# A diffusion layer on one core: where the sums of weight blocks and two sets of squares are kept and issued

## The chip, the cores and the metric

One core of a Trainium2 chip. The time is the device time of one execution, in microseconds (us), as the median of several runs. A profile is one further execution, with every instruction's start and duration on each engine: TensorE (PE, with its weight loads PEld), VectorE (DVE), ScalarE (ACT), GpSimd (POOL) and the queue of SyncE (SP), which issues most DMAs.

## The reference

One layer of a hybrid diffusion model in fp32: 1024 latent tokens of width 1024, and 256 context tokens that are only read by the latents. Cut to what matters:

```python
x = x + 0.5 * ml[2] * swiglu(modulate(rms_norm(x, norm1_g), ml[0], ml[1]), ffn1_w_in, ffn1_w_out)   # first half step
hx = modulate(rms_norm(x, norm2_g), ml[3], ml[4])
bg, cg, vc, q, k, v, gt = split(hx @ w_in)                       # mixers
y = bg * short_conv(cg * vc, conv_w)
o = attention(rope(rms_norm(q)), rope(rms_norm(k)), v)           # over context and latents
x = x + ml[5] * (sigmoid(g_conv) * (y @ w_bc) + sigmoid(g_attn) * (o @ w_ba)) @ w_out
x = x + 0.5 * ml[8] * swiglu(modulate(rms_norm(x, norm3_g), ml[6], ml[7]), ffn2_w_in, ffn2_w_out)   # second half step
return rms_norm(x, final_g)
```

`swiglu(h, a, b)` is `(silu(h @ a1) * (h @ a2)) @ b` with an inner width of 2816; `ml[i]` are shifts, scales and gates worked out from `silu(c)`. The context tokens `cx` go through the first half step and the keys and values as well.

## The kernel before

**Precision.** Every large product is taken in parts: an operand is cast on ACT to a high part (type fp32r), and DVE subtracts it from the operand for the low part (`split`, line 197). Three matmuls then stand for one: high by high, high by low, low by high.

**Fast products.** The three large products with many columns (ffn1_w_in, the mixers' w_in, ffn2_w_in) and the two with ffn1_w_out and ffn2_w_out use Winograd's form of Strassen's scheme: seven half-sized products, numbered 1 to 7, in place of eight. Their operands are blocks of weights and activations, and sums of such blocks.

*Class `Winograd` (line 491)* does the first three. The activations' operands (`r`, r1 to r7 and r0) are made by `norm0` (line 529, for the first 512 tokens, C0) and `norm1` (line 556, for the second 512, C1; temporaries `nt`, `h22` and `h12`). The weights' operands come from the generator `lefts` (line 617): for each pair of weight column blocks it loads two blocks `a` and `b` (tiles `raw`, a ring of three), makes the sums s1 = b0 + b1, s2 = s1 - a0, s3 = a0 - b0 and later a1 - s2 on POOL, and splits each into a tile of the ring `wl` (four). `prefetch` keeps four such operands ahead of PE.

Products 1 and 2 need only C0, so `start` (line 702) takes them for the first 9 pairs while `norm1` is still at work. Their results u (product 1) and c (products 1 + 2) lie in one tile of the ring `wh`, which has four buffers (`W_BUFS`). The pairs 0 and 1 (`RESIDENT` = 2) stay in it; the others are written to DRAM by `put_aside` (line 716) and loaded back by `fetch` (line 754), one pair ahead of `next_first`. After that every pair takes products 6, 7, 4, 5 and 3 (`second`, `third`), whose results DVE adds to u, v and b. The first half step does the same with its own `start_by_half`.

*`row_products` (line 820)* does the products with the second weights. It runs the seven products in the order 2, 1, 4, 6, 5, 7, 3; each goes through the 11 blocks of rows in six groups (k = 0, 2, ... 10). The right operands (`rh`, `rl`) are split from the blocks of the hidden values (`hid`), the left ones from weights (`raw`) or from weight sums (`ws`) that are built in place by DMAs with addition, issued by POOL (`plus`). In product 3 both operands lie in the rings `wl` and `wh`. After each group and at each product's end a callback `after(i, k)` is called; for the first half step it is `after1` (line 1271). When a set of four rows of `x` is complete, `done` in it writes them to DRAM and calls `mix.square` (line 545) on each: ACT squares the tile into `sq`, and DVE adds it to the accumulator `sq_acc`, from which the next norm's factor is made. `mix.accs` keeps one accumulator for C0 and one for C1.

**Rings.** `ttile` (line 116) gives a tile of 512 fp32 columns from the ring with tag t, which has 11 buffers. `rh`, `rl`, `sq`, `sq_acc`, `nt`, `h22`, `u`, `c`, `v`, `b`, `y`, the sums s1 to s3 and the tiles of the modulation (`rawm`, `macc`) all come from it. PE's results go to banks: five with tag s (`ps`), two with tag t (`pt`), one with tag o (`po`).

**Order.** The kernel is written as straight code, and the framework's planner lays each engine's queue out with a model of the durations: among the instructions that are ready, the one that stands first in the code goes first, and a new tile waits for a free buffer. Instructions marked with `strict` or `pinned` keep the order of the code on their engine. On the chip every engine then works through its queue strictly in that order.

All operations pass through one helper at line 90, so the profile shows L90 nearly everywhere; operations are told apart by the names of their tiles.

Of the kernel before, what the change touches and what calls it, by code (L numbers as in the profile page):

```python
# [9 lines left out]
F32 = mybir.dt.float32  # L10
# [8 lines left out]
P = 128  # L19
# [16 lines left out]
C0, C1, CC = ("l", 0, 512), ("l", 512, 512), ("c", 0, CT)  # L36

A_BUFS = 38
W_BUFS = 4
# [7 lines left out]
RESIDENT, AH2, AH3 = 2, 9, 9  # L47
# [4 lines left out]
def tile_dit_layer(  # L52
# [48 lines left out]
    wpool = ctx.enter_context(tc.tile_pool(name="wpool", bufs=5))  # L101
# [7 lines left out]
    def uniq(s):  # L109
        n_tiles[0] += 1  # L110
        return f"{s}_{n_tiles[0]}"

    def atile(name, shape=(P, SLOT), dt=F32):
        return apool.tile(list(shape), dt, tag="A", name=uniq(name))

    def ttile(name, n=512, dt=F32):
        t = tpool.tile([P, 512], dt, tag="t", name=uniq(name))
        return t[:, :n]
# [13 lines left out]
    def matmul(out, w, x, start, stop, pinned=False, on=False):  # L132

        inst = pe.matmul(out, w, x, start=start, stop=stop, skip_group_check=on)
        if pinned:
            tc.keep_in_program_order(inst)
# [7 lines left out]
    def load(out, in_, pinned=False):  # L144
        inst = sp.dma_start(out=out, in_=in_)
        if pinned:
            tc.keep_in_program_order(inst)
# [49 lines left out]
    def split(src, hi, lo, lo_eng=None, hi_eng=None):  # L197

        if hi_eng is dve:
            dve.tensor_copy(out=hi, in_=src)  # L200
        else:
            act.copy(out=hi, in_=src)
        (lo_eng or dve).tensor_sub(out=lo, in0=src, in1=hi.bitcast(F32))
# [177 lines left out]
    def norm_gain(name, m, gname):  # L381

        g = {}
        for s in "l" if m >= 5 else "lc":
            g[s] = const.tile([P, 8], F32, name=f"{name}_{s}")
            part_gain(g[s], m, gname, s, 0, 8)
        return g
# [77 lines left out]
    def run(steps, n=None):  # L465

        if n is None:
            for _ in steps:
                pass
        else:  # L470
            for _ in range(n):
                next(steps, None)
# [18 lines left out]
    class Winograd:  # L491
# [125 lines left out]
        def lefts(self, pairs, side_from):  # L617

            def cols(src):
                t = wpool.tile([P, SLOT], F32, tag="raw", name=uniq("raw"), bufs=3)  # L620
                load(t[:].rearrange("p (k n) -> p k n", n=P), src.rearrange("(k p) n -> p k n", p=P))
                return t[:, :512], t[:, 512:]

            def half_cols(src, half):
                t = wpool.tile([P, SLOT], F32, tag="raw", name=uniq("raw"), bufs=3)[:, :512]
                src = src[half * 512 : (half + 1) * 512]
                load(t.rearrange("p (k n) -> p k n", n=P), src.rearrange("(k p) n -> p k n", p=P))
                return t

            def parts(src):  # L630
                tag = "wh" if self.side_from and self.n_left < 2 * n + 4 and self.n_left % 2 else "wl"
                self.n_left += 1
                t = wpool.tile([P, 2, 512], F32R, tag=tag, name=uniq(tag), bufs=W_BUFS)
                strict[0] = bool(self.side_from) and self.n_left <= 2 * BY_HALF
                split(src, t[:, 0], t[:, 1], self.lo_eng)
                strict[0] = False
                return t

            n = self.n_ahead
            m = BY_HALF if self.side_from else 0  # L640
            for t in self.halves[:m]:
                yield parts(t)
            for a, _ in pairs[:m]:
                yield parts(half_cols(a, 1))
            for a, _ in pairs[m:n]:
                yield from map(parts, cols(a))
            for j, (wa, wb) in enumerate(pairs):
                side = side_from is not None and j >= side_from
                a, b = cols(wa), cols(wb)
                s1, s2, s3 = ttile("s1"), ttile("s2"), ttile("s3")  # L650
                pool.tensor_add(out=s1, in0=b[0], in1=b[1])
                pool.tensor_sub(out=s2, in0=s1, in1=a[0])
                pool.tensor_sub(out=s3, in0=a[0], in1=b[0])
                if j >= n:
                    yield from map(parts, a)
                yield parts(s2)
                yield parts(s3)
                if side:
                    yield parts(b[0])
                yield parts(b[1])  # L660
                yield parts(s1)
                pool.tensor_sub(out=s2, in0=a[1], in1=s2)
                yield parts(s2)
                if side_from is not None and j == side_from - 1:
                    for wa, wb in pairs[:side_from]:
                        yield from map(parts, cols(wa) + cols(wb))

        def prefetch(self, n, lo_engines=(None, None)):
            while len(self.ready) < n:
                self.lo_eng = lo_engines[len(self.ready) % 2]  # L670
                w = next(self.source, None)
                if w is None:
                    break
                self.ready.append(w)
# [27 lines left out]
        def start(self, norm):  # L702

            for i in range(self.n_ahead):
                t = wpool.tile([P, 2, 512], F32, tag="wh", name=uniq("uc"), bufs=W_BUFS)
                u, c = t[:, 0], t[:, 1]
                act.copy(out=u, in_=self.product(1))
                run(norm, 1)
                dve.tensor_add(out=c, in0=u, in1=self.product(2))
                if i < RESIDENT:  # L710
                    self.started.append((u, c))
                else:
                    self.put_aside(t)
            run(norm)

        def put_aside(self, t):
            ucd = dram.tile([P, 2, 512], F32, name=uniq("ucd"))
            sp.dma_start(out=ucd[:], in_=t[:])
            self.started.append(ucd)
# [308 lines left out]
    def column_pairs(w, offsets):  # L1028
        return [tuple(w[:, o : o + P] for o in ab) for ab in offsets]
# [40 lines left out]
    for k in range(4):  # L1070
# [7 lines left out]
        half1.keep(1, k, h0[k][:, 0])  # L1078
    start = half1.start_by_half()
    run(start, 1)  # L1080
    for k in range(4):
        xt = turned(t0, k + 4, ps_o if k % 2 else ps_t)
# [122 lines left out]
    for j in range(NH):  # L1205
        half1.side = side(j) if j >= SIDE_FROM else None
        u, c = half1.next_first()
# [26 lines left out]
    for d in range(0, KD, 2):  # L1234
        t = ttile("cx")
# [23 lines left out]
    mix = Winograd(xs, None, modl, 3, column_pairs(wi, mix_offsets), plain=True, ahead=AH2)  # L1259
# [8 lines left out]

    residual = {(2, 4): (C0, 0), (1, 6): (C0, 4), (4, 8): (C1, 0), (6, 4): (C1, 4)}

    def after1(i, k):
        def done(ds, ch):
            for d in ds:
                sp.dma_start(out=xd[d, :, ch[1] : ch[1] + 512], in_=xs(d, ch))
                mix.square(d, ch)

        if (i, k) in residual:
            ch, d0 = residual[i, k]
            for d in range(d0, d0 + 4):
                sp.dma_start(out=xs(d, ch), in_=xd[d, :, ch[1] : ch[1] + 512])  # L1280
        if (i, k) == (5, 0):
            gain2.update(norm_gain("gain2", 3, "g2"))
            mix.gain = gain2["l"]
        if k == NH // 2:
            if i == 1:
                done(range(4), C0)
            elif i == 7:
                done(range(4, KD), C0)
                run(norms2, 1)
                done(range(4, KD), C1)  # L1290
            elif i == 3:
                done(range(4), C1)
        if i == 3 and k in (0, 4):
            run(norms2, 1)

    row_products(ffn1_w_out[0], hs, add1, after1)


# [19 lines left out]
    for i in range(KD):  # L1318
        u = atile("u")
# [57 lines left out]
    for kt in range(10):  # L1377
        ch = CC if kt < 2 else C0 if kt < 6 else C1
# [270 lines left out]
    u = units[0]  # L1649
# [127 lines left out]
    for j in range(NH):  # L1777
        if j > 1:
            run(last_steps, 3)
        u, c = fast.next_first()  # L1780
# [82 lines left out]
```

## Time and profile before

| | us |
|---|---|
| median of 3 runs | 2678.27 |
| lowest and highest run | 2674.46 and 2678.47 |
| profiled execution | 2677.21 |
| its span, first to last instruction | 2675.3 |
| PE busy | 2637.8 |
| DVE busy | 2007.0 |
| ACT busy | 1172.3 |
| POOL busy | 557.1 |

A timeline's row gives the start in us from the span's start, the duration, the engine, the operation, `out<-in` by the program's tile names, the shape and the count; in brackets stands the engine's idle time before it and what ended it. Where several instructions of a kind follow one another, a row merges them. A row on waits gives the total, the number of waits and the longest. A row of a stretch gives its length and what each engine was busy in it, with the number of instructions that touch it. Matmuls overlap in the pipeline, so the booked duration of one (0.39 us) is longer than the pitch from one start to the next.

### The profile page before, as it was taken

The page shows a single profiled execution, that of the slowest core. Times are in us where ns is not written, and L with a number is a line of the kernel's source. Part 1 is how long each engine was busy: PE and PEld are TensorE (multiplying, and loading weights), DVE is VectorE, ACT ScalarE, POOL GpSimd, SP SyncE. Part 2 cuts the span into 40 slices and gives each one's busy share as a digit, 9 for nine tenths or more (in the row PEclk, how much of TensorE's full clock was granted, in tenths as well). Part 3 has the DMA queues.
Part 4 walks back from the last instruction along what each step waited for, and adds up shares of the span by engine and source line. Part 5 has one row for each costly group of instructions (what it writes and reads, how often), then busy time and mean ns, then how long its engine had stood idle before and what let it go on. Part 6 is the DMA issues. An engine that isn't in the chain of part 4 may idle for free.

```text
span 2675.3 us, 36939 instructions
## 1 busy us (share of the span) xinstructions
PE 2637.8 (99%) x13373; PEld 2222.0 (83%) x13373; DVE 2007.0 (75%) x3356; ACT 1172.3 (44%) x2317; POOL 557.1 (21%) x449
## 2 busy tenths in 40 slices
PE   8999999999999999999999999999999999999998
PEld 6787799888778878888999888888888788888888
DVE  5788976788877899877588676685458876667885
ACT  6532454333453643333355576574236333334443
POOL 0134201211010044332033122141001442320200
PEclk9999999999999999999999999999999999999999
DMA  8566475345974345332522432113524543228841
GB/s 316 196 190 191 141 227 165 108 131 197 300 188 110 114 157 173 114 126 79 201 66 94 91 95 61 35 42 99 164 87 146 181 153 93 89 87 284 189 90 64
DMA packets 369744, 376.93 MB, mean 141 GB/s; under 512 B 19334, under 2 KB 258072, under 8 KB 369560
## 3 DMA queue, kind: packets, MB, share of 16 engines
q1 hardware_dynamic: 358744, 353.03, 40.7%
q0 software_dynamic: 10816, 21.53, 4.9%
q8 instruction: 105, 1.72, 0.3%
q14 instruction: 79, 0.65, 0.1%
HBM read 306.78 MB, written 67.67 MB: 140 GB/s over the span
## 4 chain that ended last, share of the span: by engine, by line
PE 92%; DVE 4%; issue 1%; DMA 1%; ACT 1%; POOL 0%; SPq 0%; DVEq 0%; POOLq 0%; ACTq 0%
PE ps L90 76%; PE po L90 8%; PE pt L90 8%; DVE r L90 1%; DVE wl L90 1%; DVE nt L90 0%; DVE macc L90 0%; DMA rawm<-in_w_mod_dram 0%; DVE uc L90 0%; POOL s L90 0%; DMA raw<-in_ffn_w_in_dram 0%; DMA ws<-in_ffn_w_out_dram 0%; DVE v L90 0%; DVE y L90 0%; DMA mcol<-mrow 0%
## 5 line engine op out<-in xcount | busy, mean ns | idle before, releaser
L90 PE MATMUL ps<-r,wl 128*128 128x512 f32 x5196 | 1206.9, 391 | 10.6 <-DVE wl L90 5.2
L90 PEld LDWEIGHTS ps<-r,wl 128*128 128x128 f32 x5196 | 973.6, 188 | 220.1 <-DVE wl L90 7.7
L90 ACT CAST wl<-s 128x512 fp32r<-128x512 f32 x254 | 156.8, 620 | 322.2 <-PE ps L90 225.1
L90 POOL TENSOR_TENSOR s<-raw 128x512 f32<-128x512 f32 x64 | 91.9, 1436 | 891.3 <-DMA raw<-in_ffn_w_in_dram 583.5
L90 ACT CAST wl<-raw 128x512 fp32r<-128x512 f32 x287 | 177.5, 620 | 219.1 <-PE ps L90 157.6
L90 DVE TENSOR_TENSOR wl<-raw,wl 128x512 fp32r<-128x512 f32 x287 | 202.4, 706 | 62.5 <-ACT wl L90 59.7
L90 DVE TENSOR_TENSOR wl<-s,wl 128x512 fp32r<-128x512 f32 x254 | 230.7, 909 | 18.3 <-ACT wl L90 16.9
L90 POOL TENSOR_TENSOR s<-raw,s 128x512 f32<-128x512 f32 x64 | 103.9, 1624 | 363.2 <-DVE wl L90 363.2
L90 DVE SCALAR_TENSOR_TENSOR macc<-rawm,silu_c,macc 128x512 f32<-128x512 f32 x178 | 149.7, 858 | 12.5 <-DMA rawm<-in_w_mod_dram 11.7
L90 PE MATMUL ps<-wh,r 128*128 128x256 f32 x768 | 141.6, 284 | 0.0
L90 DVE TENSOR_TENSOR u<-u,ps 128x512 f32<-128x512 f32 x174 | 118.3, 680 | 29.0 <-PE ps L90 28.9
L90 DVE TENSOR_TENSOR pts<-pt,pts 128x512 fp32r<-128x512 f32 x160 | 108.7, 687 | 40.8 <-ACT pts L90 39.0
L90 ACT CAST pts<-pt 128x512 fp32r<-128x512 f32 x160 | 93.3, 595 | 86.5 <-PE pt L90 82.6
L90 ACT CAST rh<-hid 128x512 fp32r<-128x512 f32 x132 | 81.3, 620 | 109.5 <-PE ps L90 94.5
L90 DVE TENSOR_REDUCE m<-ps 128x1 f32<-128x512 f32 (+1 forms) x192 | 110.3, 595 | 24.1 <-PE ps L90 20.4
L90 PE MATMUL ps<-rh,wl 128*128 128x512 f32 x360 | 123.1, 392 | 2.8 <-ACT rh L90 2.8
L90 PEld LDWEIGHTS ps<-wh,r 128*128 128x128 f32 x768 | 120.8, 192 | 0.7 <-issue 0.6
L90 ACT CAST wh<-raw 128x512 fp32r<-128x512 f32 (+1 forms) x85 | 67.9, 801 | 102.1 <-PE ps L90 71.8
L90 PE MATMUL po<-pts,vh 128*128 128x512 f32 x256 | 110.0, 435 | 0.2 <-ACT pts L90 0.2
L90 PE MATMUL ps<-wl,r 128*128 128x256 f32 x384 | 109.0, 284 | 0.0
L90 DVE TENSOR_TENSOR rl<-hid,rh 128x512 fp32r<-128x512 f32 x132 | 90.1, 686 | 22.8 <-PE ps L90 13.4
L90 PE MATMUL ps<-kl,qs 128*128 128x512 f32 x384 | 104.2, 395 | 0.0
(314 smaller groups left out, 5117.4 us busy)
## 6 DMA issues: line engine op xcount, KB each, us to landing
raw<-in_ffn_w_in_dram SPq DMA_DIRECT2D x130, 512.0 KB
raw<-in_ffn_w_out_dram SPq DMA_DIRECT2D x72, 512.0 KB
raw<-in_w_in_dram SPq DMA_DIRECT2D x61, 512.0 KB
rawm<-in_w_mod_dram SPq DMA_DIRECT2D x104, 256.0 KB
hid<-hd SPq DMA_DIRECT2D x40, 512.0 KB
rawm<-in_w_mod_dram SPq DMA_DIRECT2D x32, 512.0 KB
ws<-in_ffn_w_out_dram POOLq DMA_DIRECT2D x30, 512.0 KB, 6.5
ucd<-uc SPq DMA_DIRECT2D x25, 512.0 KB
```

The lines of the kernel that those rows point to most:

```text
L90: inst = getattr(self.engine, name)(*args, **kw)
```

## The change

Three edits.

1. `sum_tiles` is new. Where `side_from` is None, that is in the mixers and in the second half step, the sums s1, s2 and s3 of a pair are no longer three tiles of the t ring. They lie in two tiles of the ring `wh` (each has room for two of them). The first half step keeps the t ring.
2. `start` puts all nine pairs u and c aside in DRAM, none stays in `wh`, and at its end it fetches the first pair into two tiles of the t ring. `next_first` then fetches one pair ahead as before.
3. In `after1`, half of the squares are no longer issued at their product's end. Those of rows 0 to 3 for C0, complete with product 1, and those of rows 4 to 7 for C1, complete with product 7, go on a list, and one is issued after each of the groups k = 2, 4, 6 and 8 of the next product (number 4, and number 3).

```diff
-                s1, s2, s3 = ttile("s1"), ttile("s2"), ttile("s3")
+                s1, s2, s3 = self.sum_tiles(j)
...
+        def sum_tiles(self, j):
+
+            if self.side_from is not None:
+                return ttile("s1"), ttile("s2"), ttile("s3")
+            s1, s23 = (wpool.tile([P, 2, 512], F32, tag="wh", name=uniq("sum"), bufs=W_BUFS) for _ in range(2))
+            return s1[:, 0], s23[:, 0], s23[:, 1]
...
                 dve.tensor_add(out=c, in0=u, in1=self.product(2))
-                if i < RESIDENT:
-                    self.started.append((u, c))
-                else:
-                    self.put_aside(t)
+                self.put_aside(t)
             run(norm)
+            self.fetch()
...
+    squares = []
+
     def after1(i, k):
         def done(ds, ch):
             for d in ds:
                 sp.dma_start(out=xd[d, :, ch[1] : ch[1] + 512], in_=xs(d, ch))
-                mix.square(d, ch)
-
+                if (d < 4) == (ch == C0):
+                    squares.append((d, ch))
+                else:
+                    mix.square(d, ch)
+
+        if squares and i in (4, 3) and k in (2, 4, 6, 8):
+            mix.square(*squares.pop(0))
```

## The prediction

> **What bounds the kernel now.** I read the page first, then the waits of TensorE (PE), then the timeline of each engine around the long ones. The page's first rows:
>
> ```profile
> span 2675.3 us, 36939 instructions
> PE 2637.8 (99%) x13373; PEld 2222.0 (83%) x13373; DVE 2007.0 (75%) x3356; ACT 1172.3 (44%) x2317; POOL 557.1 (21%) x449
> ```
>
> PE is idle for 2675.3 - 2637.8 = 37.5 us of the whole span. No edit of the change removes a matmul, so all that it can win are PE's waits, and only where it acts: the first output product (with ffn1_w_out), the start of the mixers' product behind it, and the start of the second half step. PE's waits between 690 and 1010 us, then those between 2020 and 2440 us (columns: total us, times, longest):
>
> ```profile
> PE ps L90 <- DVE wl L90: 3.2, 2, 2.8
> PE ps L90 <- ACT rh L90: 2.8, 1, 2.8
> PE pt L90 <- DVE rl L90: 1.8, 2, 1.4
> ...
> PE ps L90 <- ACT r L90: 1.6, 1, 1.6
> PE ps L90 <- DVE wl L90: 0.9, 1, 0.9
> ```
>
> The steady loops between have none: the next rows are the stretches 1010 to 1250 us and 2095 to 2440 us (PE, PEld, DVE, ACT and POOL busy, granted clock, DMA share, GB/s).
>
> ```profile
> 1010.00:1250.00 240.00, 240.00 (x1061) 198.30 (x1060) 199.00 (x285) 78.13 (x134) 85.23 (x58) 1.00 0.39 125
> 2095.00:2440.00 345.00, 345.00 (x1523) 285.25 (x1522) 239.75 (x327) 113.96 (x189) 110.04 (x77) 1.00 0.41 129
> ```
>
> So whatever the new place of the sums does in the steady loops, PE gets nothing from it there. What remains is one wait on `rh`, and the two starts.
>
> **Part 1, the squares.** The wait on `rh` lies where the output product numbered 1 ends and number 4 begins; there `after1` issues four squares at once. PE's timeline, then ScalarE's (ACT):
>
> ```profile
> 741.57 0.39 PE L90 MATMUL ps<-rh,wl 128*128 128x512 f32 x1
> 744.80 1.20 PE L90 MATMUL ps<-rh,wl 128*128 128x512 f32 x4 [2.84 <-ACT rh L90]
> 745.94 0.80 PE L90 MATMUL ps<-rl,wl 128*128 128x512 f32 x1
> 746.53 0.63 PE L90 MATMUL ps<-rh,wl 128*128 128x512 f32 x1
> 746.96 0.63 PE L90 MATMUL ps<-rl,wl 128*128 128x512 f32 x1
> ...
> 735.11 0.62 ACT L90 CAST wl<-raw 128x512 fp32r<-128x512 f32 x1 [4.74 <-DMA raw<-in_ffn_w_out_dram]
> ...
> 742.05 0.62 ACT L90 CAST wl<-raw 128x512 fp32r<-128x512 f32 x1 [0.67 <-PE ps L90]
> 742.57 1.66 ACT L90 ACTIVATE sq<-x 128x512 f32<-128x512 f32 x3
> 744.14 1.12 ACT L90 CAST rh<-hid 128x512 fp32r<-128x512 f32 x2
> ```
>
> ACT stood idle for 4.74 us before 735.11 and still did not cast the first `rh` of product 4 until the squares were done. The squares need `x`, which exists only after product 1; `sq` and `rh` come from one ring of 11 buffers (tag t). I read this as the new tile's buffer being given out behind those of the squares. Where no squares stand between two products, the casts run on through the boundary, one per step (product 6 into 5):
>
> ```profile
> 806.17 0.62 ACT L90 CAST rh<-hid 128x512 fp32r<-128x512 f32 x1 [1.58 <-PE ps L90]
> 808.89 0.62 ACT L90 CAST rh<-hid 128x512 fp32r<-128x512 f32 x1 [1.58 <-PE ps L90]
> ```
>
> At full speed one matmul follows another by about 0.23 us (the steady stretch above: 240.00 / 1061 = 0.226). PE lost 744.80 - 741.57 - 0.23 = 3.00 us by the wait. Behind it the pitch was 0.43 us (746.53 to 746.96), and the clock says why:
>
> ```profile
> 745.90:749.40 3.50, 3.50 (x9) 2.79 (x9) 3.50 (x6) 2.89 (x6) 1.21 (x1) 0.51 1.02 307
> 952.00:960.00 8.00, 4.56 (x17) 2.44 (x16) 7.92 (x13) 4.26 (x8) 1.85 (x1) 1.00 0.29 104
> ```
>
> At a granted clock of 0.51 for 3.50 us, half the speed was lost: 3.50 x 0.49 = 1.7 us. Together 4.7 us. The second row holds a wait of almost the same length (2.79 us, below) with the clock at 1.00: such a tail can fall or not, so 1.7 us either way belongs to the range. [...]
>
> What the edit saves: at least, if only ACT's queue gets shorter, 744.14 - 742.57 = 1.6 us; at most all 4.7 us. I take 4.7, nearest to the row at 806.17. The moved work, in each of two products, is four squares on ACT at 0.55 us (1.66 for three) and three additions on VectorE (DVE) at 0.68 us (a row of the same form, `uc<-uc,ps`, stands below). It lies under work that leaves room (products 4 and 3):
>
> ```profile
> 756.00:766.00 10.00, 10.00 (x46) 8.27 (x45) 6.57 (x9) 4.81 (x8) 2.28 (x3) 1.00 0.96 256
> 766.00:776.00 10.00, 10.00 (x46) 8.29 (x45) 2.74 (x5) 2.18 (x5) 1.22 (x1) 1.00 1.05 269
> 878.00:884.00 6.00, 6.00 (x36) 5.25 (x36) 4.09 (x9) 1.45 (x3) 0.00 (x0) 1.00 0.01 3
> ```
>
> With that cover gone a set would cost PE its 4 x 0.55 = 2.2 us on ACT, with the 2.0 us on DVE beside them. At the end of product 7 PE doesn't wait today, and product 3 takes no `rh` from the ring (both its operands are in wl and wh): nothing there.
>
> Late next is the chain of added DMAs for product 6. GpSimd (POOL) issues them one behind the other; two of them:
>
> ```profile
> 746.64 1.21 POOL L90 DMA_DIRECT2D ws<-in_ffn_w_out_dram  x1 [10.86 <-ACT ws L90]
> 754.91 1.22 POOL L90 DMA_DIRECT2D ws<-in_ffn_w_out_dram  x1 [7.06 <-PE ps L90]
> ```
>
> The first waits for ACT's copy of `ws`, which stands behind the squares, the second for PE: both move forward with PE. If neither did, all 4.7 us would come back as waits in product 6; I take 0, since both rows name a releaser that gets earlier.
>
> **Part 2, the sums in wh and no resident pairs.** Per weight pair POOL still does four sums of the same size, so neither POOL's nor DVE's work changes. Three to six of the 11 t buffers come free; against that, u and c of the first two pairs, until now resident in wh, take four t buffers, and each of the two starts gets two more stores (512 KB) and four more loads (256 KB) on SP's queue, at 0.34 to 0.38 us of issue each (rows of such loads stand at the last rival): six, some 2.2 us. Do the starts wait for t buffers? POOL at the mixers' start and behind it, then PE's and DVE's rows there:
>
> ```profile
> 944.69 1.47 POOL L90 TENSOR_TENSOR s<-raw 128x512 f32<-128x512 f32 x1 [123.48 <-DMA raw<-in_w_in_dram]
> ...
> 977.80 1.28 POOL L90 TENSOR_TENSOR s<-raw 128x512 f32<-128x512 f32 x1 [3.80 <-DVE v L90]
> ...
> 955.67 1.89 PE L90 MATMUL ps<-r,wl 128*128 128x512 f32 x7 [2.79 <-DVE wl L90]
> 999.51 1.66 PE L90 MATMUL ps<-r,wl 128*128 128x512 f32 x6 [0.42 <-DVE wl L90]
> ...
> 932.00:942.00 10.00, 10.00 (x46) 8.29 (x45) 10.00 (x18) 7.11 (x13) 0.00 (x0) 1.00 0.55 178
> 942.00:952.00 10.00, 10.00 (x46) 8.29 (x45) 9.93 (x15) 6.08 (x11) 5.48 (x3) 1.00 0.65 209
> ```
>
> The first sum waited for its weights' DMA, not for a buffer. DVE is full (10.00 and 9.93 of 10) with the second half's norm, and the needed low part `wl` merely stands behind that. Later sums did wait for a t buffer (977.80, for a `v`); of that PE felt 0.42 us, which I count as saved. In the second half step:
>
> ```profile
> 2077.57 0.50 PE L90 MATMUL ps<-r,wl 128*128 128x512 f32 x1 [1.61 <-ACT r L90]
> ...
> 2071.11 4.08 DVE L90 TENSOR_TENSOR r<-nt,r 128x512 fp32r<-128x512 f32 x3
> 2078.76 0.68 DVE L90 TENSOR_TENSOR uc<-uc,ps 128x512 f32<-128x512 f32 x1
> ```
>
> The same picture: DVE without a gap, three subtractions taking 4.08 us. Nothing in the edit makes DVE's work less, so 0 there. Bounds of part 2: all waits of both starts gone, 2.8 + 0.4 + 1.6 + 0.9 = 5.7 us gained (the smaller ones left aside), or the loss of the last rival.
>
> **The sum.** 4.7 + 0.4 = 5.1 us. The profiled execution took 2677.21 us (span 2675.3 and 1.9 around it): 2672.1 us. It lies 1.1 us under the median of the three runs, 2678.27, which themselves spread over 4 us.
>
> **Rivals.** *Half a gain* (0.20): the cast of `rh` is held by something else than the buffers, or the waits come back in product 6, where PE already loses 1.8 us to `rl`. Against: the rows at 806.17. It gives 2677.2 - 1.6 to 3.0, about 2675.
>
> *Buffers were the cause in the starts* (0.18): with a free t ring the order is planned anew, the low parts come ahead of the norm's, and the starts run dry no more. For it: POOL's wait for `v`. Against: DVE's full rows. 2672.1 - 5.3 = 2666.8 us. [...]
>
> *The change doesn't matter* (0.07): the new plan trades waits; 2677.
>
> *Slower* (0.13): the first pair's u comes too late. Today DVE adds to it in place; now the load needs a t buffer when the norm holds most, and DVE's in-order queue stands behind it. Today's first loads of such a pair at the two starts, the use at the mixers' start, and a load of weights:
>
> ```profile
> 2070.65 0.34 SPq L90 DMA_DIRECT2D u<-ucd  x1
> ...
> 968.98 0.38 SPq L90 DMA_DIRECT2D c<-ucd  x1
> 963.94 0.68 DVE L90 TENSOR_TENSOR uc<-uc,ps 128x512 f32<-128x512 f32 x1
> 940.82 0.37 SPq L90 DMA_DIRECT2D raw<-in_w_in_dram  x1
> ```
>
> If the new loads went out no sooner, c would land at 968.98 + 3.9 = 972.9 (3.9 from the load at 940.82 to POOL's start at 944.69), and DVE would stand 9.0 us, the `wl` subtractions behind it too. Of this PE, with five ps banks at 2.72 us a product (12 x 0.226) from 955.67, feels what lies past 969.3: from 3.6 us to all 9.0, and perhaps 1.7 us of half clock. It decides once the load lands over 5 us late. In the middle, 6.3 + 1.7 = 8.0 at each of the two starts: 2672.1 + 16 = 2688 us. Against it: the first pair is stored long before, and in the second half step even today's load, of a later pair, goes out at 2070.65, ahead of the use at 2078.76.
>
> **Chances.** The forecast has 0.42, with its own range 2669 to 2676. What a measurement can tell from no change is 0.2%, 5.4 us: faster means under 2672.9, which cuts through the forecast (0.25 on the faster side, 0.17 on the other) and touches the half gain (0.02). Faster 0.25 + 0.02 + 0.18 = 0.45; same 0.17 + 0.18 + 0.07 = 0.42; slower 0.13. The range 2664 to 2684 leaves out half of the slower case and the ends of the third.
>
> **What would show it.** Right: no PE wait on ACT `rh` between products 1 and 4, `rh` casts ahead of the boundary, no stretch at half clock there, squares among product 4's casts. Waits on `wl` and `r` at the two starts about as long as now. Wrong: a wait of the same size in product 6; DVE idle ahead of `u<-u,ps` with a DMA as releaser; a PE wait in either steady loop; or the starts clear of waits.

## The result and the profile after

| | before | after |
|---|---|---|
| median of 20 runs, us | 2678.32 | 2672.53 |
| lowest and highest run, us | 2672.91 and 2683.98 | 2668.84 and 2677.77 |
| profiled execution, us | 2677.21 | 2670.08 |

The ratio of after to before is 0.998, with a 95% interval of 0.9973 to 0.9987: faster by 3.5 to 7.2 us. The forecast was 2672.1 us.

The head of the page of the changed kernel:

```profile
span 2668.3 us, 36840 instructions
PE 2633.8 (99%) x13373; PEld 2220.0 (83%) x13373; DVE 2002.0 (75%) x3356; ACT 1173.6 (44%) x2317; POOL 558.4 (21%) x449
```

The number of matmuls is the same. PE's waits in the changed kernel, first from 690 to 1010 us, then from 2020 to 2440 us:

```profile
PE ps L90 <- DVE r L90: 2.5, 2, 2.0
PE ps L90 <- DVE rl L90: 1.9, 1, 1.9
PE pt L90 <- ACT wl L90: 1.2, 1, 1.2
PE pt L90 <- DVE wl L90: 0.4, 1, 0.4
...
PE ps L90 <- DVE r L90: 0.5, 1, 0.5
PE ps L90 <- DVE wl L90: 0.5, 1, 0.5
```

The 2.8 us on `rh` are gone. The largest waits that are left have other names than before: 1.9 us on `rl` in product 6, where before had two of 1.8 us in sum, and 2.5 us on `r` in two waits at the mixers' start, where before had one of 2.8 us on `wl`. And one wait is new. It lies in the steady loop from 1010 us on, where the kernel before had none:

```profile
1017.02 1.20 PE L90 MATMUL ps<-r,wl 128*128 128x512 f32 x4 [1.51 <-DVE wl L90]
```

The prediction had named a wait there as a sign of being wrong. A second profile of the same kernel has 0.3 us at this place.

The boundary of products 1 and 4 on the timeline of the changed kernel, PE and then ACT:

```profile
741.36 0.39 PE L90 MATMUL ps<-rh,wl 128*128 128x512 f32 x1
...
744.08 0.39 PE L90 MATMUL ps<-rh,wl 128*128 128x512 f32 x1
...
736.11 0.62 ACT L90 CAST rh<-hid 128x512 fp32r<-128x512 f32 x1
...
737.15 0.62 ACT L90 CAST rh<-hid 128x512 fp32r<-128x512 f32 x1
...
745.04 0.62 ACT L90 ACTIVATE sq_acc<-x 128x512 f32<-128x512 f32 x1
745.56 1.12 ACT L90 CAST rh<-hid 128x512 fp32r<-128x512 f32 x2
...
748.06 0.63 ACT L90 ACTIVATE sq<-x 128x512 f32<-128x512 f32 x1
748.60 0.60 ACT L90 CAST rh<-hid 128x512 fp32r<-128x512 f32 x1
```

`rh` for product 4 is now cast at 736.11 and 737.15, ahead of the last matmul of product 1 (741.36), and the squares stand one by one among the casts of product 4. The same stretch as before at the clock:

```profile
745.90:749.40 3.50, 3.50 (x17) 2.92 (x16) 3.50 (x7) 3.30 (x6) 0.71 (x1) 1.00 1.08 305
```

17 matmuls at a granted clock of 1.00, where before had 9 at 0.51.

**One ruler for all runs.** Each profile has 13,373 matmuls, and product follows product in the same order, so the start of the n-th can be compared between kernels. (Up to where the two plans part, DVE's first 914 and ACT's first 553 instructions stand in the same order before and after, by the names of their tiles, though their starts differ by up to 2.0 us.) Counted from 0, number 3708 is the last of product 1 and number 3720 lies in product 4. In the kernel before, 3720 is this row (3708 is the row at 741.57 in the prediction):

```profile
749.09 0.51 PE L90 MATMUL ps<-rh,wl 128*128 128x512 f32 x1
```

From 3708 to 3720 before took 749.09 - 741.57 = 7.53 us (unrounded) and after 744.08 - 741.36 = 2.72 us: 4.81 us less. In the same way the table gives, for four stretches, how much longer (+) or shorter (-) a kernel was than before, in us. They end at number 3720 (boundary), at 3912 (into product 6; before at 795.09), at 4920 (the rest of the output product and the mixers' start; before at 1024.35), and, from 10329 to 10608, at the start of the second half step (before from 2020.02 to 2085.26).

| profile | boundary | products 4 to 6 | mixers' start | second half step's start |
|---|---|---|---|---|
| after | -4.81 | -0.25 | +1.03 | -2.34 |
| after, second profile | -4.81 | +1.29 | +0.15 | -1.29 |
| squares alone | -4.81 | +3.12 | -0.91 | -0.01 |
| first set of squares alone | -4.81 | +1.20 | -0.88 | +0.50 |
| sums in wh and all aside | -1.44 | +1.97 | +0.71 | -2.35 |
| all aside alone | -0.22 | -1.10 | -0.94 | -0.76 |
| sums in wh alone | -0.09 | -0.03 | +5.63 | +1.89 |
| squares and all aside | -4.81 | -0.46 | -0.74 | -0.77 |
| same, rows of x later | -4.81 | -2.48 | -0.78 | -0.77 |
| after, rows of x later | -4.81 | -1.57 | +1.54 | -2.31 |
| after, sums in order | -4.81 | -0.16 | +3.52 | +0.09 |
| after, t ring of 10 | -4.81 | +3.96 | +1.02 | +1.33 |
| sq in its own ring, t of 10 | -2.75 | +6.94 | +6.73 | +1.33 |

The first row sums to -6.4 us; with -0.36 us elsewhere the last matmul comes 6.7 us earlier. Each row is one execution. Outside these stretches executions differ too: the second profile of the changed kernel was 1.9 us behind before's when product 1 ended, the first 0.2 us ahead. So the medians judge a whole kernel, the table says where.

Among the profiles with a t ring of 11, the clock parts the column of products 4 to 6. Four of them have a stretch of 3.4 us at half clock behind a wait in product 6, and these four lost time: the changed kernel's second profile, the squares alone, the first set alone, and the sums in wh and all aside (+1.20 to +3.12). The others have none there and lost nothing (-2.48 to -0.03). The two profiles of the changed kernel show it best. Their waits on `rl` are 1.93 and 1.87 us; behind them stand, in the first and in the second profile:

```profile
771.90:775.40 3.50, 3.50 (x17) 2.89 (x16) 3.50 (x6) 2.19 (x4) 1.21 (x1) 1.00 0.11 13
774.10:777.60 3.50, 3.50 (x10) 2.69 (x10) 3.35 (x6) 2.18 (x4) 1.21 (x1) 0.51 0.18 18
```

At almost the same wait, the second profile is 1.29 + 0.25 = 1.54 us longer in this column.

### The profile page after: what moved, and what is told of

It is laid out like the page before. It is cut to its first block, busy times and chain, and to the rows that moved or that the text cites. A ratio compares the mean times of both kernels' runs of the same rounds, so it can differ in the third digit from the quotient of the medians.

```text
span 2668.3 us, 36840 instructions
## 1 busy us (share of the span) xinstructions
PE 2633.8 (99%) x13373; PEld 2220.0 (83%) x13373; DVE 2002.0 (75%) x3356; ACT 1173.6 (44%) x2317; POOL 558.4 (21%) x449
## 4 chain that ended last, share of the span: by engine, by line
PE 90%; DVE 5%; DMA 2%; issue 1%; ACT 1%; POOL 1%; SPq 0%; DVEq 0%; POOLq 0%; ACTq 0%
PE ps L90 74%; PE po L90 8%; PE pt L90 8%; DVE wl L90 1%; DVE r L90 1%; DMA raw<-in_ffn_w_in_dram 1%; DVE nt L90 0%; DMA rawm<-in_w_mod_dram 0%; DMA ws<-in_ffn_w_out_dram 0%; DVE u L90 0%; DVE macc L90 0%; POOL s L90 0%; DVE y L90 0%; POOL sum L90 0%; DVE sq_acc L90 0%
## 5 line engine op out<-in xcount | busy, mean ns | idle before, releaser
L90 ACT CAST wl<-sum 128x512 fp32r<-128x512 f32 x168 | 103.2, 620 | 231.9 <-PE ps L90 184.9
L90 DVE TENSOR_TENSOR wl<-sum,wl 128x512 fp32r<-128x512 f32 x168 | 152.2, 908 | 17.8 <-ACT wl L90 16.8
L90 POOL TENSOR_TENSOR sum<-raw 128x512 f32<-128x512 f32 x42 | 60.6, 1443 | 497.9 <-DMA raw<-in_w_in_dram 203.2
L90 DVE TENSOR_TENSOR u<-u,ps 128x512 f32<-128x512 f32 x186 | 126.2, 680 | 33.6 <-PE ps L90 33.6
L90 POOL TENSOR_TENSOR sum<-raw,sum 128x512 f32<-128x512 f32 x42 | 62.0, 1476 | 268.7 <-DVE wl L90 261.8
L90 POOL TENSOR_TENSOR s<-raw 128x512 f32<-128x512 f32 x22 | 32.0, 1457 | 378.5 <-DMA raw<-in_ffn_w_in_dram 297.1
```

The costliest lines, as they stand in the source:

```text
L90: inst = getattr(self.engine, name)(*args, **kw)
```

## The experiments

Edits are shown against the kernel before unless the sentence says "against after". Intervals are 95%, against the kernel before on the same chip.

**The squares alone** (`e1_squares`): the third edit of the change on the kernel before.

> The kernel before with the third edit alone (the spread squares). Theory of the forecast: the two halves of the change act apart. The wait of 2.84 us on rh between products 1 and 4 and the stretch at half clock behind it go, the same matmul of product 4 starts 4.6 us earlier than before, and this lead is kept to the end; product 6's waits (0.55 and 1.54 us before, one of 2.09 us after) sum to about 2.1 us in either form; both starts run as before. Time about 5 us under before, some 2673.5 us. Rival 1: it was the t ring made free by the sums that let the casts run ahead; then the wait on rh stays and the time is before's, 2678. Rival 2: without the other edits the chain of added DMAs gives the gain back in product 6; then a wait of some 4 to 5 us lies there and the time is about 2677.

Median 2674.51 us against 2677.76, ratio 0.9992 with an interval of 0.9983 to 1.0001. The boundary gained 4.81 us to the hundredth, so rival 1 falls: the free t ring isn't needed. But this profile gave 3.12 us back in products 4 to 6: one wait of 3.7 us on `rl`, where before had two of 1.8 us in sum, and half clock behind it. Rival 2 is partly right. By the medians the gain was 3.2 us, not 5, and the interval just reaches no gain at all.

**The sums and the pairs without the squares** (`e2_sums`), against after:

```diff
-                if (d < 4) == (ch == C0):
-                    squares.append((d, ch))
-                else:
-                    mix.square(d, ch)
+                mix.square(d, ch)
```

> The changed kernel with the squares issued at once again, so only the sums in the ring wh and the pairs all put aside. Theory of the forecast: wait on rh 2.8 us and half clock behind it as before, 0.4 us gained at the mixers' start, nothing in the second half step: 2677.9 us. What the trace of the changed kernel suggests instead: 1.0 us lost at the mixers' start and 2.1 us gained at the start of the second half step, 1.1 us in all, about 2677.2 us; these two should be seen here at the same size if they come from these edits. Rival: the free t ring alone clears the boundary of products 1 and 4 too; then the time is near 2672.5.

Median 2676.87 us, ratio 1.0 (0.9991 to 1.0009). The wait on `rh` is back, 2.84 us, yet the boundary is 1.44 us shorter than before. The clock behind the wait is the reason. PE's timeline in this run, and the stretch behind the wait:

```profile
744.11 1.19 PE L90 MATMUL ps<-rh,wl 128*128 128x512 f32 x4 [2.84 <-ACT rh L90]
```

```profile
744.00:747.50 3.50, 3.39 (x14) 2.55 (x15) 3.50 (x6) 3.50 (x7) 1.21 (x1) 1.00 0.93 236
```

The clock stayed at 1.00. In the run with only the pairs put aside (below), the same wait had the half clock behind it (timeline, then stretch):

```profile
743.70 2.08 PE L90 MATMUL ps<-rh,wl 128*128 128x512 f32 x4 [2.84 <-ACT rh L90]
```

```profile
743.40:746.90 3.50, 3.20 (x8) 2.54 (x9) 3.41 (x6) 3.50 (x6) 1.21 (x1) 0.51 0.91 268
```

Of four profiles with this wait, three have half clock behind it (before, all aside alone, sums in wh alone) and one hasn't. The two starts moved as the trace of the changed kernel had suggested, +0.71 and -2.35 us.

**A ring of their own for the squares** (`e3_own_ring`):

```diff
-    tpool = ctx.enter_context(tc.tile_pool(name="tpool", bufs=11))
+    tpool = ctx.enter_context(tc.tile_pool(name="tpool", bufs=10))
+    sqpool = ctx.enter_context(tc.tile_pool(name="sqpool", bufs=1))
...
-            sq = ttile("sq" if n else "sq_acc")
+            sq = ttile("sq_acc") if n in (0, KD - 1) else sqpool.tile([P, 512], F32, tag="q", name=uniq("sq"))
```

> The kernel before, squares issued at once, but the tiles sq (all but the first and the last of each set of eight) come from a ring of their own with one buffer; the t ring has 10 buffers in place of 11 to make the room. Theory of the forecast (the order of buffers in the t ring puts rh behind the squares): only the first square, whose tile sq_acc still comes from t, stands ahead of the first cast of rh; the casts interleave with the other squares, and the wait falls from 2.84 us to some 1.2 to 1.7 us (three squares of 0.55 us less); whether the clock halves behind it is open, so 1.2 to 3.3 us are gained there. Rival (the burst of four squares in ScalarE's queue sets the wait, whatever the ring): the wait stays at 2.8 us. With one t buffer less small waits may come elsewhere; I look at the boundary first and at the total, about 2676 us by the theory, second.

Median 2701.90 us, ratio 1.0098 (1.0083 to 1.0113): the whole is 24 us slower, but the boundary, which was the question, shortened by 2.75 us. PE and ACT there:

```profile
752.68 1.19 PE L90 MATMUL ps<-rh,wl 128*128 128x512 f32 x4 [1.75 <-ACT rh L90]
...
751.50 0.62 ACT L90 ACTIVATE sq_acc<-x 128x512 f32<-128x512 f32 x1
752.03 0.60 ACT L90 CAST rh<-hid 128x512 fp32r<-128x512 f32 x1
752.54 0.62 ACT L90 ACTIVATE sq<-x 128x512 f32<-128x512 f32 x1
753.07 0.60 ACT L90 CAST rh<-hid 128x512 fp32r<-128x512 f32 x1
```

`rh` stands right behind `sq_acc`, the one square whose tile still comes from t, and ahead of the others, although in the code all four come first. The wait is 1.75 us, just over what the ring theory gave, and not the 2.8 us of the rival. The own ring's buffer was still unused when `rh` went ahead of the first `sq`, so that ring's being short doesn't explain the order. So the order of the buffers in t did hold the cast behind the squares. The 24 us lie elsewhere. This profile was already 9.0 us behind before at number 3708, as the other run with a t ring of 10 was (9.45 us, below); later the largest waits are 9.2 us at the mixers' start and 6.2 us in product 6. That all of it comes from the shorter t ring is likely, but not shown.

**The first set of squares alone** (`e4_first_set`): as the squares alone, with another condition.

```diff
-                if (d < 4) == (ch == C0):
+                if d < 4 and ch == C0:
```

> The kernel before with only the squares of rows 0 to 3 of the first 512 tokens spread over product 4; those of rows 4 to 7 of the second 512 tokens, at the end of product 7, are issued at once as before. Theory: product 3 takes no rh from the t ring, so the second set never cost anything; the gain is the same as with both sets spread, some 5 us (2673.5 us). Rival: each set is worth a part; then this one gains clearly less than the run with both, by 1 us or more.

Median 2673.93 us, ratio 0.9985 (0.9976 to 0.9995), beside 2674.51 us with both sets. The set at product 7 is worth nothing measurable, as the theory had it.

**All pairs aside** (`e5_all_aside`): the second edit of the change alone.

> The kernel before with the middle edit alone: all nine pairs put aside in DRAM, the first one fetched into the t ring at the end of the start, the sums still in the t ring, squares at once. Theory: the gain of 2.1 us at the start of the second half step comes from the t buffers that the sums no longer hold; here u and c of the first pair take two t buffers more instead, so that gain is absent or turns into a loss of up to some 5 us at each start, and the time is 2678 to 2685 us. Rival 1: the gain there comes from the pairs put aside; then the start of the second half step is again 2.1 us shorter here, and the total about 2676. Rival 2 (the slower case of the forecast): the reload of the first pair is late by itself; then VectorE waits on a DMA ahead of u<-u,ps at both starts, 8 us each.

Median 2674.95 us, ratio 0.999 (0.9981 to 0.9999). The feared loss isn't there. The second half step's start gained 0.76 us: more than the theory's nothing, less than the 2.1 us of rival 1, so neither has the whole. Rival 2 falls: nothing is 8 us late at either start. By the medians this edit alone brings 3.2 us (0.3 to 5.1 by the interval), as much as the squares alone. Its profile has 1.10 us of that in products 4 to 6, and 0.94 us at the mixers' start, where the squares alone gained 0.91 us.

**A t ring of 10 in the changed kernel** (`e6_t10`), against after:

```diff
-    tpool = ctx.enter_context(tc.tile_pool(name="tpool", bufs=11))
+    tpool = ctx.enter_context(tc.tile_pool(name="tpool", bufs=10))
```

> The changed kernel with 10 buffers in the t ring in place of 11. In the kernel before, a run with 10 and an own ring for sq lost some 24 us, 7 to 9 of them in one wait at the mixers' start (9.4 us). Theory: with the sums out of the ring the starts have buffers to spare; the waits at both starts stay within 2 us of the changed kernel's, and what is lost lies in the first half step and in the output product, whose sums and operands still use the t ring: some 5 to 15 us in all, 2678 to 2688 us. Rival: the starts are as tight as before; then a wait of 7 us or more stands at the mixers' start again.

Median 2693.14 us, ratio 1.0056 (1.0043 to 1.007): 15 us over before, more than forecast. At number 3708 this profile was already 9.45 us behind before, and products 4 to 6 lost 3.96 us. At the mixers' start it lost no more than the changed kernel with 11 (+1.02 against +1.03), where the run with an own ring lost 6.73 us. So with the sums out, the mixers' start has a t buffer to spare, and the first half step hasn't.

**The rows of x later** (`e7_rows_later`), against after:

```diff
-    residual = {(2, 4): (C0, 0), (1, 6): (C0, 4), (4, 8): (C1, 0), (6, 4): (C1, 4)}
+    residual = {(2, 4): (C0, 0), (1, 6): (C0, 4), (6, 2): (C1, 0), (5, 0): (C1, 4)}
...
+            strict[0] = ch == C1
             for d in range(d0, d0 + 4):
-                sp.dma_start(out=xs(d, ch), in_=xd[d, :, ch[1] : ch[1] + 512])
+                (pool if ch == C1 else sp).dma_start(out=xs(d, ch), in_=xd[d, :, ch[1] : ch[1] + 512])
+            strict[0] = False
```

> The changed kernel, with the eight loads of rows of x for the second 512 tokens moved out of product 4: they are issued on GpSimd's queue, four behind the sums of group 4 of product 6 (callback at k = 2) and four at the start of product 5, in place of SyncE's queue during product 4. Theory: the wait of 1.9 to 3.9 us in product 6 comes from the added DMAs of GpSimd's chain, which take 8 to 10 us instead of 6 to 6.5 while the loads of x share the DMA engines; without them the chain's steps stay near 6.5 us, the wait shrinks by 2 us or more, and the time falls to 2670 us or below. Rival 1: the chain is slow by itself (one added DMA at a time, 6.2 us for a group that PE needs 5.4 us for): the wait stays at 2 us. Rival 2: the eight issues on GpSimd, 1.2 us each, hold back its own chain and give a new wait in products 6 or 5: slower than the changed kernel.

Median 2671.16 us, ratio 0.9974 (0.9964 to 0.9983). The wait in product 6, first on the timeline of the changed kernel (PE, ACT, POOL), then the view of its DMA issues for the added DMA of 256 KB issued between 756 and 770 us, the last column being the time from issue to landing:

```profile
771.10 0.50 PE L90 MATMUL ps<-rl,wl 128*128 128x512 f32 x1 [1.93 <-DVE rl L90]
...
768.58 0.63 ACT L90 ACTIVATE ws<-ws 128x512 f32<-128x512 f32 x1 [8.83 <-DMA ws<-in_ffn_w_out_dram]
...
757.43 2.15 POOL L90 DMA_DIRECT2D ws<-in_ffn_w_out_dram  x2 [7.52 <-DMA raw<-in_ffn_w_out_dram]
766.68 1.22 POOL L90 DMA_DIRECT2D ws<-in_ffn_w_out_dram  x1 [7.11 <-issue]
```

```profile
ws<-in_ffn_w_out_dram POOLq DMA_DIRECT2D x1, 256.0 KB, 10.3
```

PE is named as waiting for DVE's `rl`, but DVE and ACT had stood still for the DMA: ACT 8.83 us until `ws` landed. That PE feels it at this matmul comes from the order on DVE. Here is this `rl` with the subtraction that needs the DMA, in the changed kernel and then before:

```profile
769.75 0.69 DVE L90 TENSOR_TENSOR wh<-ws,wh 128x512 fp32r<-128x512 f32 x1 [7.62 <-ACT wh L90]
770.36 0.68 DVE L90 TENSOR_TENSOR rl<-hid,rh 128x512 fp32r<-128x512 f32 x1
...
766.44 0.68 DVE L90 TENSOR_TENSOR rl<-hid,rh 128x512 fp32r<-128x512 f32 x1
774.99 0.69 DVE L90 TENSOR_TENSOR wh<-ws,wh 128x512 fp32r<-128x512 f32 x1 [7.26 <-ACT wh L90]
```

Before, this `rl` was made ahead of the wait for the DMA, now behind it. With a t ring of 11, all eight profiles with spread squares have the new order and the four others the old one, in which PE waits later in product 6. What the order costs by itself isn't shown. With the eight loads of `x` elsewhere, the same two views, and PE's waits between 745 and 830 us:

```profile
756.68 2.15 POOL L90 DMA_DIRECT2D ws<-in_ffn_w_out_dram  x2 [6.91 <-DMA raw<-in_ffn_w_out_dram]
762.66 1.22 POOL L90 DMA_DIRECT2D ws<-in_ffn_w_out_dram  x1 [3.83 <-DVE sq_acc L90]
```

```profile
ws<-in_ffn_w_out_dram POOLq DMA_DIRECT2D x1, 256.0 KB, 8.6
```

```profile
PE pt L90 <- DVE rl L90: 0.5, 1, 0.5
```

The chain's step falls from 766.68 - 757.43 = 9.25 to 5.98 us, and of PE's wait 0.5 us are left, 1.4 us less where 2 or more were expected. The theory stands for the wait. But the long step isn't new: in the kernel before it took 9.28 us (POOL's rows at 762.85 and 772.13), so moving the loads is a gain of its own, not a repair of the change. The total is 1.4 us under the changed kernel's 2672.53; its own two sets of runs differ by 0.9 us, so that alone shows little.

**The sums in the order of the code** (`e8_sums_in_order`), against after:

```diff
+                strict[0] = side_from is None
                 pool.tensor_add(out=s1, in0=b[0], in1=b[1])
                 pool.tensor_sub(out=s2, in0=s1, in1=a[0])
                 pool.tensor_sub(out=s3, in0=a[0], in1=b[0])
+                strict[0] = False
```

> The changed kernel with the sums s1, s2, s3 held in the order of the code on GpSimd. In the kernel before every pair's sums run s1, s2, s3; in the changed kernel, where s2 and s3 share a tile, they run s1, s3, s2 in the mixers and the second half step, although product 6 needs s2 first. Theory: that swap makes s2 some 1.7 us later (one sum's duration) and is the cause of the new wait of 1.7 us near 1015 us and of part of those at both starts; with the order restored that wait goes and 1.5 to 4 us are gained: 2669 to 2671 us. Rival: the releaser there is the weights' DMA for s1, which the order doesn't move; the waits stay and the time is the changed kernel's, 2672.5 us.

Median 2673.69 us, ratio 0.9984 (0.9975 to 0.9993). The theory falls: the order was restored, and the waits at the mixers' start grew from 4.0 to 4.6 us in sum. PE's waits from 945 to 1030 us in this run, where the changed kernel had 2.5 us on `r` and 1.5 us on `wl`:

```profile
PE ps L90 <- DVE wl L90: 2.4, 2, 2.1
PE ps L90 <- DVE r L90: 2.2, 1, 2.2
```

The rival has the releaser right: POOL's first sum ahead of the wait near 1016 us waited 4.19 us for its weights' DMA, and 4.29 us in the changed kernel.

**The sums in wh alone** (`e9_sums_in_wh`): the first edit alone, the pairs 0 and 1 resident.

> The kernel before with the first edit alone: the sums in the ring wh, the pairs 0 and 1 resident there as before, squares at once. Theory after eight runs: this is the edit that costs; between 70 and 95 us behind the mixers' start, where the runs with the sums in wh lost 1.3 to 4 us against before and the run with all pairs aside and the sums in t lost nothing, 1 to 4 us are lost here too, and the start of the second half step keeps its long wait (1.8 and 0.5 us): 2679 to 2681 us. Rival: the loss in the mixers comes only where sums and put-aside pairs meet; then no loss here, 2678 us or less.

Median 2683.43 us, ratio 1.002 (1.0011 to 1.0029): 5.65 us slower than before. PE and POOL at the two starts:

```profile
973.98 0.84 PE L90 MATMUL ps<-r,wl 128*128 128x512 f32 x2 [1.98 <-ACT wl L90]
2074.65 5.88 PE L90 MATMUL ps<-r,wl 128*128 128x512 f32 x13 [3.13 <-ACT wl L90]
...
971.75 1.53 POOL L90 TENSOR_TENSOR sum<-sum,raw 128x512 f32<-128x512 f32 x1 [5.31 <-DVE uc L90]
2071.07 1.40 POOL L90 TENSOR_TENSOR sum<-sum,raw 128x512 f32<-128x512 f32 x1 [1.01 <-DMA ucd<-uc]
```

POOL's sum waits until a pair's tile `uc` is done with, once for DVE's work on it (5.31 us) and once for its store. Two sums and two resident pairs fill all four buffers of `wh`.

**The change without its first edit** (`e10_sums_in_t`), against after:

```diff
-                s1, s2, s3 = self.sum_tiles(j)
+                s1, s2, s3 = ttile("s1"), ttile("s2"), ttile("s3")
```

> The changed kernel without its first edit: the sums stay in the t ring, the pairs are all put aside and the squares are spread. Theory: the gains of the other two edits add up (boundary of products 1 and 4 some 4.7 us, of which product 6 takes none to 3 back; start of the second half step 1 to 2 us) and the loss of 1 to 2 us in the mixers goes: 2670.5 to 2672.5 us, not slower than the changed kernel. Rival: the sums in the t ring hold back the spread squares or u and c of the reloaded pairs; slower than the changed kernel, 2673 us or more.

Median 2672.92 us, ratio 0.9982 (0.9973 to 0.999), a little over the theory's range; the changed kernel in the same session had 2673.43 us. The first edit is worth nothing measurable on top of the other two.

**The same, with the rows of x later** (`e11_rows_later_too`): the edit of `e7_rows_later` on the kernel just shown.

> As the run with the sums in t, and with the eight loads of rows of x on GpSimd's queue behind product 6's sums. Theory: product 6's wait shrinks to under 1 us as it did in the changed kernel with the same move; 1 to 2 us under the run with the sums in t, 2669 to 2671 us, the lowest time of all. Rival: the two don't add; the same time as the changed kernel with that move, 2671.2 us, or more.

Median 2669.66 us, ratio 0.9971 (0.9959 to 0.9982), the lowest of all: 8.1 us under before and 3.8 us under the changed kernel of the same session. The stretch that held product 6's wait, first in the changed kernel, then here:

```profile
766.00:776.00 10.00, 8.07 (x37) 6.33 (x35) 6.25 (x10) 4.88 (x9) 2.44 (x2) 1.00 0.66 141
```

```profile
766.00:776.00 10.00, 10.00 (x46) 8.29 (x45) 8.40 (x13) 3.34 (x7) 1.23 (x2) 1.00 0.64 128
```

PE is busy throughout, with 46 matmuls in place of 37. Whether the moved loads or the sums kept in t make the step from the changed kernel to this one isn't parted by the medians; the run with the sums in t alone had no lead.

**The changed kernel again** (`e12_after_again`), unedited.

> The changed kernel once more, unedited, for a second profile. At the start of the second half step four profiles of different kernels have two waits of 0.82 and 0.65 us and five have waits of 1.77 and 0.5 us; no single edit parts them. If the plan of the kernel decides, this profile has 0.82 and 0.65 us again, within 0.1 us. If it is decided anew in each execution (GpSimd's sum and VectorE's subtractions getting in each other's way), the long form may show. The wait in product 6 is expected between 1.2 and 3.9 us. Time 2672.5 us.

Median 2673.43 us, ratio 0.9984 (0.9975 to 0.9992). Product 6's wait is 1.87 us, within what was expected. The second half step's start differs from the first profile of the very same kernel. POOL, DVE and PE there, first profile:

```profile
2067.18 2.47 POOL L90 TENSOR_TENSOR sum<-raw 128x512 f32<-128x512 f32 x1 [4.04 <-DMA raw<-in_ffn_w_in_dram]
...
2066.62 1.88 DVE L90 TENSOR_TENSOR r<-nt,r 128x512 fp32r<-128x512 f32 x3
...
2071.96 1.21 PE L90 MATMUL ps<-r,wl 128*128 128x512 f32 x4 [0.55 <-DVE r L90]
```

Second profile:

```profile
2069.89 1.30 POOL L90 TENSOR_TENSOR sum<-raw 128x512 f32<-128x512 f32 x1 [4.00 <-DMA raw<-in_ffn_w_in_dram]
...
2069.37 4.08 DVE L90 TENSOR_TENSOR r<-nt,r 128x512 fp32r<-128x512 f32 x3
...
2075.84 0.50 PE L90 MATMUL ps<-r,wl 128*128 128x512 f32 x1 [1.60 <-ACT r L90]
```

POOL's sum took 2.47 us and DVE's three subtractions 1.88 us in the first profile, 1.30 us and 4.08 us in the second. The second is the picture of the kernel before (1.40 and 4.08 us). Over the whole start the two profiles of one kernel differ by 2.34 - 1.29 = 1.05 us.

## Why the prediction was right, and where it wasn't

**The squares, 4.7 us: right in size and cause.** The boundary shortened by 4.81 us in all nine profiles with spread squares. That the cast stood behind the squares through the buffers' order is shown by the own ring, where only the square that still used t stayed ahead of it. That the clock's share can fall or not, 1.7 us either way, came as written: the same 2.84 us gave a clock of 0.51 in one run and 1.00 in another. In these runs the length of the wait alone didn't decide it: half clock followed the wait of 2.84 us in three profiles and one of 1.87 us in product 6 of the changed kernel's second profile, and none followed one of 1.93 us there in its first. What decides it, no run shows.

**The moved squares under products 4 and 3, 0 us: right** as far as the boundary's stretch and the first set alone can show; no wait of PE in the profile after names a square as its cause. But the order of DVE's work in product 6 did change with them (above).

**Late next, the chain of added DMAs, 0 us: right for the chain, wrong for the term.** The chain did move forward with PE, as both quoted releasers promised. ACT's copy of `ws` that ends the long wait in product 6 starts 773.82 - 749.09 = 24.73 us behind matmul 3720 before and 768.58 - 744.08 = 24.50 us behind it in the changed kernel, and PE's waits there sum to 1.8 and 1.9 us. What the term left out is the half clock behind such a wait, which the prediction had counted at the boundary alone. It came in three of the six profiles with spread squares, a t ring of 11 and the loads in place, and these gave 1.2 to 3.1 us back; the other three gave none. The squares alone lost the most because their wait was longer too (3.7 us), as there one step of the chain took 10.1 us in place of 8.2 to 8.7; the reason for that stays open. In medians the squares alone brought 3.2 us. Moving the loads of `x` shortened the wait to 0.5 us in one kernel and removed it in the other.

**Part 2, 0.4 us and no effect on the starts: a fair size, from a wrong step.** The 0.42 us at 999.51 that I credited to free buffers don't belong to the edits: the mixers' stretch is 0.7 to 0.9 us shorter in all five runs with the sums still in t and the ring of 11, the squares alone among them. So most likely it was that one execution of the kernel before that had them. The medians put the two edits together at 0.9 us, with an interval of the ratio of 0.9991 to 1.0009, 2.4 us either way. What I didn't see is that the two edits belong together: the sums in `wh` alone cost 5.65 us, since they and the resident pairs fill that ring, and putting the pairs aside makes the room. I had costed part 2 as one piece and only counted t buffers; the ring into which the sums move has four buffers, and I never added up who holds them. Nor was it right that PE gets nothing from the sums' new place in the steady loops. In the mixers' loop behind 1010 us, all six profiles with the sums in `wh` and the pairs aside have a wait on `wl`, of 0.3 to 2.1 us; where the sums stay in t, none is over 0.2 us.

**Waits at the two starts about as long as now: not right.** At the mixers' start the changed kernel's two profiles lost 1.03 and 0.15 us, at the other start they gained 2.34 and 1.29 us. Behind the longest wait at the mixers' start, 2.0 and 2.2 us, both have 3.4 us at half clock, where before's 2.79 us had none. The first of them:

```profile
958.60:962.00 3.40, 2.96 (x7) 1.82 (x6) 3.13 (x5) 1.53 (x3) 0.55 (x1) 0.50 0.27 109
```

DVE's full rows were read rightly as the limit, but how long DVE's work takes differs between profiles: I took its 4.08 us for three subtractions as given, and in the changed kernel's first profile they took 1.88 us, beside a sum of 2.47 us on POOL. What part of the gain at the second half step's start belongs to which edit stays open, beyond this: the three profiles with the pairs aside and the sums in t have 0.76 to 0.77 us of it.

**The rivals.** *Half a gain*: its second mechanism, time lost again in product 6, is real, by the clock more than by the waits, and its share varies with the execution. *Buffers in the starts*: not shown for the kernel as a whole. The starts of the changed kernel aren't free of waits, though a tenth buffer's loss no longer hurt the mixers' start. *Slower by a late reload*: falls. At the mixers' start the changed kernel's first load of u goes out at 943.34 and its use is 18.5 us later, waiting 0.24 us for PE and not for a DMA (in the second half step it goes out at 2050.58, 22.9 us ahead of its use):

```profile
943.34 0.42 SPq L90 DMA_DIRECT2D u<-ucd  x1
...
961.87 0.69 DVE L90 TENSOR_TENSOR u<-u,ps 128x512 f32<-128x512 f32 x1 [0.24 <-PE ps L90]
```

**The total, 2672.1 against 2672.5 us,** fits better than its parts, and that is luck. The boundary brought 4.8 us, products 4 to 6 gave 0.25 us more in one profile and took 1.3 us back in the other, and the two starts together gave 1.3 and 1.1 us, where the sum had 0.4.

## What to carry to other kernels

When tiles of different purposes share a ring, the ring's order is also an order of work: a tile that is asked for behind a burst of short-lived ones is made behind them, even where its engine is idle, so spread the burst or look for the wait at the boundary. Before moving tiles into another ring, list who holds that ring's buffers at the tightest moment; an edit that costs alone (here 5.65 us) can be harmless with its partner, so time both. And before a stage's gain of 1 or 2 us is explained, profile the same kernel twice: here one stage of one kernel differed by 1.05 us, and another by 1.54 us at the same wait, since the clock fell behind it in one execution and not in the other.

## What the runs showed of the hardware that was not expected

One wait of 2.84 us on PE, at the same matmul, was followed by a stretch of 3.5 us at a granted clock of 0.51 in three profiles and by none in a fourth. Shorter waits did the same: in two profiles of one kernel, a wait of 1.93 us had a clock of 1.00 behind it and one of 1.87 us a clock of 0.51.

Where a sum on GpSimd and three subtractions on VectorE lay beside each other at the start of the second half step, one of the two took longer, and which one differed between executions: sum 2.47 us and subtractions 1.88 us, or 1.30 and 4.08 us, in two profiles of one kernel. What decides it isn't shown, and their starts don't tell: the sum starts 0.56 us behind the first of the three subtractions in the one profile and 0.52 us in the other.

An added DMA of 256 KB took 10.3 us from issue to landing while eight loads of 256 KB each shared the stretch, and 8.6 us without them; with the loads PE felt that as a wait of 1.9 us on a subtraction that had itself waited for the DMA.

One buffer less in the t ring cost the changed kernel 20.6 us (2693.14 against 2672.53).
